# A strided slice copied by three DMA queues: which batches go through on-chip memory first

## The chip, the cores and the metric

The kernel runs on one core of a Trainium2 chip. The metric is the device time of one execution in microseconds. A GB/s here is the bytes that the DMA engines moved per time; a transfer from HBM to HBM counts its bytes once.

## The reference

```python
def setup_inputs():
    batch, seq, dim = 32, 1024, 512
    return {"x": np.random.randn(batch, seq, dim).astype(np.float32),
            "start": 0, "stop": 512, "stride": 2}

def reference(x, start, stop, stride):
    return x[:, start:stop:stride, :].astype(np.float32)
```

Of each of 32 batches the even rows among the first 512 are copied: 256 rows of 512 floats, 2 KB each, 512 KB per batch and 16.78 MB in all. The rows taken from x lie 4 KB apart; in the output they lie one after the other. Nothing is computed, so the kernel is made of DMA transfers alone.

## The kernel before

The 256 output rows of a batch are taken in pairs, which gives two halves of 128 rows each: the even rows (parity 0) and the odd rows (parity 1). One half goes straight from x to the output in HBM, a *direct copy*. The other half is *held*: it is loaded into a tile in SBUF with one row per partition, and stored from there. `apart(b)` gives the parity of the direct half: 1 for the first two batches of every four, 0 for the other two. The held half has the opposite parity.

Transfers are put together as follows.

- A direct copy (line 39) takes two batches, `b` and `b + step`, which have the same parity. It moves 2 x 128 rows, 512 KB. There are 16 of them, in the order of the list `copied`: for each group of eight batches the pairs (0, 5), (2, 7), (1, 4) and (3, 6).
- A load (lines 37 and 42) fills one tile, `held[i]`, with the held halves of batches 2i and 2i+1, again 512 KB. There are 16 tiles, one for each pair of batches, each with its own memory, so no tile is used twice.
- A store (line 46) writes one batch's held half from its tile, 256 KB. There are 32.

Three queues issue them, each in the written order (`manual_schedule`). SP and ACT issue the loads of tiles 0 to 5 in turn, three each (`FIRST = 6`). The gpsimd queue (POOL) issues the 16 direct copies, and after the fourth copy and each one following it one of the loads of tiles 6 to 15, until these are used up. SP then issues all stores. Their order begins with tile 13, the gate: as SP's instructions run in order, no store starts before that tile's load has landed. Tiles 0 to 12, 14 and 15 follow.

Each transfer signals a completion semaphore. The framework gives eight of them to SP and ACT together and eight to the gpsimd queue, in turn. A transfer that takes a semaphore again waits for the one that had it before. So the ninth transfer of the gpsimd queue waits for its first, and SP's stores are at most eight in flight.

Of the kernel before, what the change touches and what calls it, by code (L numbers as in the profile page):

```python
# [3 lines left out]

FIRST = 6


def apart(b):


    return 1 - (b >> 1 & 1)


def two(t, b, step, parity):

    return t[b : b + step + 1 : step].rearrange("b (p two) d -> two p b d", two=2)[parity]


def kernel(tc, x, start, stop, stride, out):

    nc = tc.nc
    src = x[:, start:stop:stride, :]
    B, rows, D = out.shape
    P = rows // 2
    sp, act, pool = nc.sync, nc.scalar, nc.gpsimd  # L30
    copied = [(g + b, step) for g in range(0, B, 8) for b, step in ((0, 5), (2, 5), (1, 3), (3, 3))]
    pairs = B // 2
    with tc.tile_pool(name="io", bufs=1) as io:
        held = [io.tile([P, 2, D], x.dtype, name=f"held{i}") for i in range(pairs)]
        with tc.manual_schedule():
            for i in range(FIRST):
                (sp, act)[i % 2].dma_start(held[i], two(src, 2 * i, 1, 1 - apart(2 * i)))
            for n, (b, step) in enumerate(copied):
                pool.dma_start(two(out, b, step, apart(b)), two(src, b, step, apart(b)))  # L39
                i = n + FIRST // 2  # L40
                if FIRST <= i < pairs:
                    pool.dma_start(held[i], two(src, 2 * i, 1, 1 - apart(2 * i)))  # L42
            order = [pairs - 3, *range(pairs - 3), pairs - 2, pairs - 1]
            for b in (2 * i + k for i in order for k in range(2)):
                to = out[b].rearrange("(p two) d -> two p d", two=2)[1 - apart(b)]
                sp.dma_start(to, held[b // 2][:, b % 2])


# [1 line left out]
_INS = ['x', 'start', 'stop', 'stride']  # L50
_OUTS = [((32, 256, 512), 'float32')]

_NUMBERS = {'start': 0, 'stop': 512, 'stride': 2}


def kernel(**inputs):
    import numpy as _np
    import concourse.bacc as _bacc
    import concourse.tile as _tile
    from concourse import mybir as _mybir  # L60
    from concourse.bass_utils import run_bass_kernel_spmd as _run

    nc = _bacc.Bacc("TRN2", target_bir_lowering=False, num_devices=1)  # L63
    arrays, args = {}, []
    for name in _INS:
        if name in _NUMBERS:
            args.append(_NUMBERS[name])
            continue
        a = _np.ascontiguousarray(inputs[name])
        if a.dtype.kind in "iu":  # L70
            a = a.astype(_np.int64)
        arrays[f"in_{name}_dram"] = a
        args.append(nc.dram_tensor(f"in_{name}_dram", a.shape, _mybir.dt.from_np(a.dtype), kind="ExternalInput").ap())
    for i, (shape, dtype) in enumerate(_OUTS):
        dt = _mybir.dt.from_np(_np.dtype(dtype))
        args.append(nc.dram_tensor(f"out_{i}_dram", shape, dt, kind="ExternalOutput").ap())
    with _tile.TileContext(nc) as tc:  # L77
        kernel(tc, *args)
    r = _run(nc, [arrays], core_ids=[0])
    got = tuple(r.results[0][f"out_{i}_dram"] for i in range(len(_OUTS)))  # L80
    return got[0]
```

## Time and profile before

| | us |
|---|---|
| median of 7 runs | 79.32 (78.46 to 80.31) |
| profiled execution, its own time | 79.26 |
| profiled execution, its span | 77.5 |

| transfers in the profile | count | KB each | issue, engine | issue to landing, median us |
|---|---|---|---|---|
| direct copies | 16 | 512 | POOL, 699 ns | 13.4 |
| loads of tiles 6 to 15 | 10 | 512 | POOL, 728 ns | 13.2 |
| loads of tiles 0, 2, 4 | 3 | 512 | SP | 11.1 |
| loads of tiles 1, 3, 5 | 3 | 512 | ACT | 12.0 |
| stores | 32 | 256 | SP, 0.33 us | 5.9 |

The span runs from the first instruction to the last; the execution's own time holds something before and after it. A transfer's issue is short, and the bytes move later on 16 DMA engines that all queues share. In the profile q0 is the gpsimd queue, q1 SP's and q10 ACT's. The share of a queue is the time that its packets took, in parts of 16 engines' time in the window; with several packets in flight the shares of a short window can add up to a little over 100%.

### The profile page before, as it was taken

How to read it: one execution, taken by the hardware profiler on the slowest of the kernel's cores; microseconds unless marked ns; L12 is line 12 of the kernel's file. 1: busy time of each engine (PE TensorE's matmuls, PEld its weight loads, DVE VectorE, ACT ScalarE, POOL GpSimd, SP SyncE). 2: the span in 40 equal slices, each digit the busy share in tenths (PEclk: the TensorE clock that was granted, in tenths of full speed). 3: DMA queues.
4: the chain of work that ended last, by engine and by line, in shares of the span. 5: the costliest groups of instructions: out<-in, count | busy, mean ns of one | idle time of the engine just before them, and what ended most of it. 6: DMA issues, size and time to landing. Idle time of an engine off the chain costs nothing.

```text
span 77.5 us, 122 instructions
## 1 busy us (share of the span) xinstructions
POOL 18.6 (24%) x30
## 2 busy tenths in 40 slices
POOL 4995003203463355054425100000000000000000
DMA  0899999999999998899999999999999999999940
GB/s 10 256 293 329 314 281 348 300 353 409 383 298 341 362 349 220 294 370 415 376 370 389 330 294 315 337 390 411 404 406 406 363 355 363 349 351 355 340 154 11
DMA packets 9984, 25.17 MB, mean 325 GB/s; under 512 B 1024, under 2 KB 1024, under 8 KB 9984
## 3 DMA queue, kind: packets, MB, share of 16 engines
q0 software_dynamic: 3744, 13.63, 50.2%
q1 hardware_dynamic: 5424, 9.96, 37.7%
q10 hardware_dynamic: 816, 1.57, 6.6%
HBM read 16.78 MB, written 16.78 MB: 433 GB/s over the span
## 4 chain that ended last, share of the span: by engine, by line
DMA 50%; issue 3%; POOLq 1%; POOL 1%; PEldq 0%
DMA held<-in_x_dram 37%; DMA out_dram<-in_x_dram 13%; POOLq L77 1%; POOL out_dram L39 1%; PEldq L77 0%
## 5 line engine op out<-in xcount | busy, mean ns | idle before, releaser
L39 POOL DMA_DIRECT2D out_dram<-in_x_dram x16 | 11.2, 699 | 12.1 <-DMA out_dram<-in_x_dram 9.6
L42 POOL DMA_DIRECT2D held<-in_x_dram x10 | 7.3, 728 | 12.0 <-DMA out_dram<-in_x_dram 7.5
L63 POOL MEMSET const-float32-0.0<- 128x1 f32 x1 | 0.1, 98 | 0.2 <-issue 0.2
L63 POOL MEMSET const-bfloat16-1.0<- 128x1 bf16 x1 | 0.1, 101 | 0.0
L63 POOL MEMSET const-float32-1.0<- 128x1 f32 x1 | 0.1, 98 | 0.0
L63 POOL MEMSET const-uint8-127<- 128x1 uint8 x1 | 0.1, 98 | 0.0
## 6 DMA issues: line engine op xcount, KB each, us to landing
out_dram<-in_x_dram POOLq DMA_DIRECT2D x16, 512.0 KB, 13.4
out_dram<-held SPq DMA_DIRECT2D x32, 256.0 KB, 5.9
held<-in_x_dram POOLq DMA_DIRECT2D x10, 512.0 KB, 13.2
held<-in_x_dram SPq DMA_DIRECT2D x3, 512.0 KB, 11.1
held<-in_x_dram ACTq DMA_DIRECT2D x3, 512.0 KB, 12.0
```

What stands on the lines that cost most here:

```text
L39: pool.dma_start(two(out, b, step, apart(b)), two(src, b, step, apart(b)))
L42: pool.dma_start(held[i], two(src, 2 * i, 1, 1 - apart(2 * i)))
L63: nc = _bacc.Bacc("TRN2", target_bir_lowering=False, num_devices=1)
L77: with _tile.TileContext(nc) as tc:
```

## The change

SP and ACT now load the first two batches of every four, a tile with 256 KB from each of them: SP takes the even batch, ACT the odd one. These are tiles 0, 2, 4 and so on to 14, all of parity 0, eight loads on each queue. The gpsimd queue starts with the eight direct copies of the other two batches of every four, also of parity 0 (the list `last`). Then it loads an odd tile and makes a direct copy from the list `first` in turn, eight times, all of parity 1. The gate of the stores is tile 11 (`gate = B - 10` is batch 22). The stores go on with tiles 0 to 10, 12 and 14, and end with 13 and 15. The stores' size, the direct copies' size and the number of both stay.

```diff
-FIRST = 6
...
+def one(t, b, parity):
+    return t[b].rearrange("(p two) d -> two p d", two=2)[parity]
...
-    copied = [(g + b, step) for g in range(0, B, 8) for b, step in ((0, 5), (2, 5), (1, 3), (3, 3))]
-    pairs = B // 2
+    first = [(g + b, step) for g in range(0, B, 8) for b, step in ((0, 5), (1, 3))]
+    last = [(g + b, step) for g in range(0, B, 8) for b, step in ((2, 5), (3, 3))]
...
+        def direct(b, step):
+            pool.dma_start(two(out, b, step, apart(b)), two(src, b, step, apart(b)))
+
+        def store(b):
+            sp.dma_start(one(out, b, 1 - apart(b)), held[b // 2][:, b % 2])
+
         with tc.manual_schedule():
-            for i in range(FIRST):
-                (sp, act)[i % 2].dma_start(held[i], two(src, 2 * i, 1, 1 - apart(2 * i)))
-            for n, (b, step) in enumerate(copied):
-                pool.dma_start(two(out, b, step, apart(b)), two(src, b, step, apart(b)))
-                i = n + FIRST // 2
-                if FIRST <= i < pairs:
-                    pool.dma_start(held[i], two(src, 2 * i, 1, 1 - apart(2 * i)))
-            order = [pairs - 3, *range(pairs - 3), pairs - 2, pairs - 1]
-            for b in (2 * i + k for i in order for k in range(2)):
-                to = out[b].rearrange("(p two) d -> two p d", two=2)[1 - apart(b)]
-                sp.dma_start(to, held[b // 2][:, b % 2])
+            for b in range(0, B, 4):
+                for k, queue in enumerate((sp, act)):
+                    queue.dma_start(held[b // 2][:, k], one(src, b + k, 1 - apart(b)))
+            for b, step in last:
+                direct(b, step)
+            for n, (b, step) in enumerate(first):
+                pool.dma_start(held[2 * n + 1], two(src, 4 * n + 2, 1, 1 - apart(4 * n + 2)))
+                direct(b, step)
+            gate = B - 10
+            order = [b for b in range(B) if b // 2 % 2 == 0 or b < gate]
+            order = [gate, gate + 1, *order]
+            for b in [*order, *(b for b in range(B) if b not in order)]:
+                store(b)
```

## The prediction

> **What bounds the kernel now.** No engine computes here. The page's busy rows come first, then its DMA queues, and only the queues carry the time.
>
> ```profile
> span 77.5 us, 122 instructions
> POOL 18.6 (24%) x30
> DMA  0899999999999998899999999999999999999940
> DMA packets 9984, 25.17 MB, mean 325 GB/s; under 512 B 1024, under 2 KB 1024, under 8 KB 9984
> q0 software_dynamic: 3744, 13.63, 50.2%
> q1 hardware_dynamic: 5424, 9.96, 37.7%
> q10 hardware_dynamic: 816, 1.57, 6.6%
> HBM read 16.78 MB, written 16.78 MB: 433 GB/s over the span
> ```
>
> The 16 DMA engines are nine tenths busy from the second slice to the second last; the three queue shares add up to 94.5%. So the time is bytes over rate, and the question is at which rate each stage moves. q0 is the gpsimd queue, q1 SP's, q10 ACT's. Second, the chain and SP's waits give the one order that binds:
>
> ```profile
> SPq L46 <- DMA held<-in_x_dram: 41.2, 1, 41.2
> SPq L46 <- DMA out_dram<-held: 14.8, 24, 3.3
> 43.37 28.21 SPq L46 DMA_DIRECT2D out_dram<-held  x32
> ```
>
> SP sits 41.2 us until held13, the gate, has landed; then it stores, eight in flight. Third, stage windows (the columns are: window, length, POOL busy, clock, DMA share, GB/s), cut where queues start or run out:
>
> ```profile
> 0.00:6.00 6.00, 4.93 (x11) 1.00 0.65 188
> 6.00:19.00 13.00, 2.98 (x5) 1.00 1.00 332
> 19.00:48.00 29.00, 10.71 (x16) 1.00 0.99 341
> 48.00:52.00 4.00, 0.00 (x0) 1.00 1.04 369
> 52.00:60.00 8.00, 0.00 (x0) 1.00 1.03 401
> 60.00:77.50 17.50, 0.00 (x0) 1.00 0.87 293
> ```
>
> Stage 1 is start-up with SP's and ACT's loads alone, stage 2 all three queues, stage 3 the gpsimd queue alone (its packets are 99% of it), stage 4 (48 to 60) stores beside its remainder, then a few us of stores alone, stage 5 stores alone with the tail. The first stores are issued at 43.4, but the queue view has 13 packets of q1 before 48. The bytes by queue in stages 2 and 3:
>
> ```profile
> q0 software_dynamic: 624, 2.30, 48.1%
> q10 hardware_dynamic: 553, 1.05, 26.3%
> q1 hardware_dynamic: 503, 0.96, 26.0%
> ...
> q0 software_dynamic: 2710, 9.88, 98.5%
> q1 hardware_dynamic: 13, 0.03, 0.2%
> ```
>
> **What the Trainium skill says.** DMA: Bandwidth & Descriptors, "Issuing engines are not separate DMA queues": queues share the same 16 engines, so spreading transfers gains only issue time. The trace agrees: shares 48.1, 26.3 and 26.0% in stage 2, sum 100%, at 332 GB/s against 341 for one queue. The same page, "Queues, rings and completion order": each engine goes round its queues packet by packet. Take off 16 small completion packets per DMA: q0's 26 DMAs leave 3328 packets for 13.63 MB, 4 KB each; q10's three leave 768 for 1.57 MB, 2 KB each. One turn each would then give gpsimd half the bytes: it had 2.30 of 4.31 MB. The same page, "Latency and other measured facts", has HBM copies that slow down at large power-of-two row pitches (half the rate at 4 MiB), and infers, unverified, that the rows then fall on the same channels. It lists pitches from 512 KiB up; the rows of one transfer here are 8 KB apart in x and 4 KB in out, and this trace has no stage where all transfers share a row half. So it says only that addresses can matter, and stays a rival.
>
> A last set of windows, in the same columns, shows how uneven a stage is inside, which the sums and rivals below need:
>
> ```profile
> 8.00:13.00 5.00, 0.73 (x1) 1.00 0.98 302
> 27.00:28.50 1.50, 0.73 (x1) 1.00 1.06 412
> 28.50:31.00 2.50, 1.42 (x2) 1.00 0.79 215
> 35.00:37.00 2.00, 0.83 (x2) 1.00 1.02 416
> 60.00:73.00 13.00, 0.00 (x0) 1.00 1.06 357
> ```
>
> The gpsimd queue alone can run at 412 to 416, and loses that in holes such as the third line, while stores alone run evenly at 357.
>
> **The change part by part.** Bytes stay: 8.39 MB direct, 8.39 loaded, 8.39 stored, 25.17 in all.
>
> (1) Two loads of 512 KB (1.05 MB) leave the gpsimd queue (24 DMAs, 12.58 MB) for SP and ACT, which load 16 x 256 KB = 4.19 MB instead of 3.15. Price by packet: q10's 6.6% x 77.5 x 16 = 82 us over 768 packets is 107 ns per 2 KB row; q0's 50.2% is 622 us over 3328, 187 ns per 4 KB, 94 per row. 512 rows x 13 ns / 16 engines = +0.4 us. This is a check on the sum below and not added to it.
>
> (2) Issue: SP and ACT issue eight instructions each instead of three, 0.33 us apiece by the stores' row, 2.7 us in all, beside 20 us of their own transfers: nothing. Loads five to eight of each queue wait for a completion semaphore, shared eight among both queues. Behind ACT's waits stands nothing; behind SP's stand the stores, which wait for the gate anyway. Four loads in flight per queue are 1.05 MB at about 78 GB/s per queue, 13 us of work, so the queue doesn't run dry. Eight more DMAs are 128 more completion packets, 8 per engine, under 0.1 us.
>
> (3) POOL now issues eight directs first, then load and direct in turn, each with the same wait for the DMA eight places before. Its instructions, 0.69 and 0.73 us, fall by two, in an engine 24% busy: nothing.
>
> (4) The gate is held11 instead of held13, but it is the nineteenth DMA of the gpsimd queue in both (eight directs, then load and direct five times, then this load; before: eleven directs and eight loads). Stores so flow when that queue has moved the same bytes: 2.30 + 9.88 = 12.18 MB at the point where stage 3 ends.
>
> (5) Stages. 1: unchanged, 6.0 us, 1.13 MB. 2: SP and ACT have 4.19 - 1.13 = 3.06 MB left, at 2.01 MB per 13 us: 19.8 us, to 25.8; gpsimd moves 2.30/13 x 19.8 = 3.50 MB beside it. 3: 12.18 - 3.50 = 8.68 MB at 341: 25.5 us, to 51.3 instead of 48. Left for gpsimd: 0.40 MB instead of 1.45. 4: in before 1.45 + 3.23 MB of stores at 391 (4.69 MB in 12 us). If the first 3.23 MB of stores keep that rate: 3.63 MB, 9.3 us, to 60.6, and the rest as before takes 17.5: 78.1, so +0.6. If the fast part ends instead with the gpsimd queue plus 4.5 us, as in before (its last packets come near 55.5): 1.6 us of mix, 4.5 us at 401, to 57.4 with 2.0 MB stored; stage 5 then has 6.39 MB instead of 5.14, and 1.25 MB at the steady 357 (60 to 73) is 3.5 us: 78.4, so +0.9. I take the middle, +0.75.
>
> (6) Cover at the gate. For some 4.6 us after the gate the stores hardly flow, and gpsimd covers it, with seven DMAs behind the gate in before, five now. By the sum 0.40 MB, about 1.2 us, is left when they flow; but the 16 engines are not level, so some may be dry earlier. Bounds 0 and +1.0 us, a gain excluded because less cover can't help; I take +0.25.
>
> Sum: +1.0 us. The profiled execution took 79.26 with a span of 77.5, so 1.76 lies around it, unchanged; 79.26 + 1.0 = 80.3. The median of the runs, 79.32, is the same to 0.1%.
>
> **The rivals.**
>
> A. Nothing to measure: bytes over rate, the same 16 engines; 79.3. For it: stages 2 and 3 differ by 3% in rate. Against: stores alone run at 357, while every window after 48 with gpsimd beside them is at 369 or more.
>
> B. Faster: the holes of stage 3 go. In before its windows range from 416 down to 215 GB/s. There loads and directs of both row halves follow each other. In the changed kernel every load and direct of stage 3 touches the second half of each row pair only (held of batches 2 and 3 of four, direct of 0 and 1), and of stage 2 the first only. If mixing the halves makes the holes, half of them gone is 375 GB/s: 8.68 MB in 23.1 instead of 25.5, -2.3, so 78.0. It wins by over 1% from 367 GB/s on. Against: holes come at a few places while the mixing is everywhere.
>
> C. Much slower, by the same addresses: with one row half in use, reads and writes fall on fewer paths. At 302 GB/s, the rate of the weakest long stretch (8 to 13 us), stages 2 and 3 with 15.24 MB take 50.5 instead of 45.3 us: +5.2, 85.2 with (5) and half of (6). For it: HBM moves one and a half bytes per queue byte in these stages, some 510 GB/s, the highest in the kernel. Against: every single DMA in before uses one half already, and gpsimd reaches 416.
>
> **How the numbers follow.** Chances: forecast 0.50, A 0.20, B 0.13, C 0.17. About 1% (78.5 to 80.1) is what a measurement can tell from no change. Of the forecast's half, 0.40 lies over 80.1 and 0.09 within; of A 0.14 within, 0.03 on either side; with C 0.60 slower, 0.23 within and B with the rest 0.17 faster. The range goes from half a gain of B, 78.2, to the middle of C, 83.5; the forecast's own range is 79.5 to 81.5.
>
> **What would show it.** Right: ACT's and SP's loads lasting to 24 to 28 us, the gate near 46.7 instead of 43.4, stage 3 at 330 to 355 GB/s, gpsimd empty by 53, and stores alone at about 357 for over 20 us. B is seen in a stage 3 over 365, C in stages 2 and 3 under 315. An idle stretch of the DMA row after the gate shows (6) too small. The prediction is wrong if stage 3's rate moves by over 5% either way, or if stores alone run at 400.

## The result: slower by 0.7%, and the profile after

The changed kernel takes 79.78 us in the median of 27 runs against 79.10 for 64 runs of the kernel before. The ratio of the two, which leaves out the slow runs of each (those over 1.5% above its fastest), is 1.0072, with a 95% interval of 1.0048 to 1.0097. That is +0.57 us (0.38 to 0.77), where +1.0 was forecast. It is clear of zero and under the 1% named as what a measurement can tell, so it falls in the "within 1%" class, not in the "slower" one that had the largest chance.

The profiled execution took 79.15 us, 0.6 below its median, while that of before, 79.26, lay 0.2 above its own. The two spans are therefore all but equal (77.4 and 77.5), and what follows reads rates, byte counts and the order of events from the profiles, and differences of time from the timed runs alone. The page after, its queues:

```profile
span 77.4 us, 128 instructions
DMA packets 10368, 25.17 MB, mean 325 GB/s; under 512 B 1152, under 2 KB 1152, under 8 KB 10368
q0 software_dynamic: 3456, 12.58, 48.3%
q1 hardware_dynamic: 5760, 10.49, 41.3%
q10 hardware_dynamic: 1152, 2.10, 7.2%
```

The bytes moved as the change says: 1.05 MB left q0, half of it for SP, half for ACT. The shares add up to 96.8% (94.5% before): the engines are as full as they were. SP's waits (us in total, times, longest) and its line of stores (start, length):

```profile
SPq L45 <- DMA held<-in_x_dram: 33.1, 2, 28.1
SPq L50 <- DMA held<-in_x_dram: 8.7, 4, 3.0
45.97 25.45 SPq L45 DMA_DIRECT2D out_dram<-held  x32
```

The first line holds the wait for the gate. The second is new: SP's loads five to eight wait for a semaphore. The third shows that no store was late by it, since stores start at 45.97 behind the gate in any case. The stage windows (window, length, POOL busy, clock, DMA share, GB/s), cut where this kernel's queues start or run out, and below the bytes by queue from 50 to 54:

```profile
6.00:25.00 19.00, 4.43 (x7) 1.00 1.04 332
25.00:50.00 25.00, 7.79 (x11) 1.00 0.99 339
50.00:54.00 4.00, 0.00 (x0) 1.00 1.02 385
54.00:60.00 6.00, 0.00 (x0) 1.00 1.06 401
60.00:73.00 13.00, 0.00 (x0) 1.00 1.07 355
...
q0 software_dynamic: 250, 0.89, 59.7%
q1 hardware_dynamic: 347, 0.65, 41.9%
```

All three queues together run at 332 GB/s and gpsimd alone at 339, the rates of before (332 and 341). The stage with three queues lasts six microseconds longer. The first 13 us of it, the stretch that it had in before, read 319. When the stores begin to flow, near 50, gpsimd has 0.92 MB left (0.89, and 0.03 after 54), against 1.45 MB at the same point of before.

### The profile page after: what moved, and what is told of

Its sections match the earlier page's. It is cut to its first block, busy times and chain, and to the rows that moved or that the text cites. A ratio compares the mean times of both kernels' runs of the same rounds, so it can differ in the third digit from the quotient of the medians.

```text
span 77.4 us, 128 instructions
## 1 busy us (share of the span) xinstructions
POOL 17.1 (22%) x28
## 3 DMA queue, kind: packets, MB, share of 16 engines
q0 software_dynamic: 3456, 12.58, 48.3%
## 4 chain that ended last, share of the span: by engine, by line
DMA 43%; POOL 6%; issue 4%; POOLq 1%; PEldq 0%
DMA out_dram<-in_x_dram 30%; DMA held<-in_x_dram 13%; POOL out_dram L42 5%; POOL held L54 1%; POOLq L89 1%; PEldq L89 0%
## 5 line engine op out<-in xcount | busy, mean ns | idle before, releaser
L54 POOL DMA_DIRECT2D held<-in_x_dram x8 | 5.8, 728 | 12.4 <-DMA out_dram<-in_x_dram 10.2
```

The costliest lines, as they stand in the source:

```text
L54: pool.dma_start(held[2 * n + 1], two(src, 4 * n + 2, 1, 1 - apart(4 * n + 2)))
```

## The experiments

Each ratio is to the kernel before on the same chip. The chips differ a little: the median of before was 79.19 beside the first four kernels, and 79.75, 79.63 and 79.64 beside the later ones.

**Which part of the change costs: the bytes, their order, or their size.** The first kernel moves the bytes and leaves the order and the size as in before. Its gate keeps the nineteenth place on the gpsimd queue, so five transfers lie behind it instead of seven:

```diff
-FIRST = 6
+FIRST = 8
-                i = n + FIRST // 2
+                i = n + FIRST // 2 - 1
-            order = [pairs - 3, *range(pairs - 3), pairs - 2, pairs - 1]
+            order = [pairs - 2, *range(pairs - 2), pairs - 1]
```

> Before, with tiles 6 and 7 moved from the gpsimd queue to SP and ACT (eight loads of 512 KB there instead of six), the gate again at the nineteenth place of the gpsimd queue (tile 14), row halves mixed as in before. Theory 1, the moved 1.05 MB: slower by the whole of what the change cost, +0.5 to +0.9 us, ratio 1.006 to 1.011. Theory 2, the order by row halves: within 0.25 us of before. Theory 3, the loads of 256 KB with their waits: within 0.25 us of before.

Measured: 1.0054 (1.0025 to 1.0084), +0.43 us. The second kernel changes the order (of loads, copies and stores) and nothing else:

```diff
-    copied = [(g + b, step) for g in range(0, B, 8) for b, step in ((0, 5), (2, 5), (1, 3), (3, 3))]
+    copied = [(g + b, step) for half in (((2, 5), (3, 3)), ((0, 5), (1, 3))) for g in range(0, B, 8) for b, step in half]
+    tiles = [0, 2, 4, 6, 8, 10, 12, 14, 1, 3, 5, 7, 9, 11, 13, 15]
...
-                (sp, act)[i % 2].dma_start(held[i], two(src, 2 * i, 1, 1 - apart(2 * i)))
+                j = tiles[i]
+                (sp, act)[i % 2].dma_start(held[j], two(src, 2 * j, 1, 1 - apart(2 * j)))
...
-                    pool.dma_start(held[i], two(src, 2 * i, 1, 1 - apart(2 * i)))
-            order = [pairs - 3, *range(pairs - 3), pairs - 2, pairs - 1]
+                    j = tiles[i]
+                    pool.dma_start(held[j], two(src, 2 * j, 1, 1 - apart(2 * j)))
+            order = [11, *range(11), 12, 14, 13, 15]
```

> Before, with the same number and size of transfers on each queue, but ordered by row half: SP and ACT load tiles 0, 2, 4, 6, 8, 10, the gpsimd queue makes the direct copies of half 0 first and then those of half 1, and loads tiles 12, 14 and then the odd ones. Gate tile 11 at the nineteenth place. Theory 1, the moved bytes: within 0.25 us of before. Theory 2, the order by row halves: +0.5 to +0.9 us. Theory 3, the 256 KB loads: within 0.25 us.

Measured: 1.0014 (0.9988 to 1.0040), nothing that can be told from before. The third takes the changed kernel and gives SP and ACT whole tiles:

```diff
-            for b in range(0, B, 4):
-                for k, queue in enumerate((sp, act)):
-                    queue.dma_start(held[b // 2][:, k], one(src, b + k, 1 - apart(b)))
+            for k, b in enumerate(range(0, B, 4)):
+                (sp, act)[k % 2].dma_start(held[b // 2], two(src, b, 1, 1 - apart(b)))
```

> After, with SP's and ACT's loads as whole tiles of 512 KB, four each in turn, instead of half tiles of 256 KB, eight each; so no load there waits for a semaphore. Theory 1 and theory 2: as slow as after, ratio 1.005 to 1.010 to before. Theory 3, the 256 KB loads and their waits cost it: back to before, ratio 0.998 to 1.003.

Measured: 1.0049 (1.0011 to 1.0086): not back at before. Nothing shows that the smaller loads and their waits cost, though the interval leaves room for a part. Theory 1 stands: the moved bytes carry 0.43 of the 0.57 us, and the rest is inside the intervals. That five transfers behind the gate cost anything by themselves is not seen below, where before has five with no byte moved.

**The dose.** If bytes on SP and ACT cost, twice as many should cost twice as much. Ten loads there (`FIRST = 10`, `i = n + FIRST // 2 - 4`, gate tile 14):

> The dose doubled: before with ten loads of 512 KB on SP and ACT instead of six (2.1 MB moved instead of 1.05), gate again at the nineteenth place of the gpsimd queue (tile 14), three transfers behind it. If each moved MB costs what the first did (+0.43 us per 1.05 MB by the run with eight): ratio 1.008 to 1.014. If only a loss that the first step brought counts, and no price per byte: 1.003 to 1.007.

Measured: 1.0119 (1.0077 to 1.0160), +0.95 us; the second step costs what the first did. Four loads (`FIRST = 4`, `i = n + FIRST // 2 + 1`, gate tile 12):

> The dose taken the other way: before with four loads on SP and ACT instead of six, so 1.05 MB more on the gpsimd queue, gate at its nineteenth place (tile 12), nine transfers behind it. If bytes on the gpsimd queue are cheaper, faster than before: ratio 0.993 to 0.998. If before stands at the best point between two costs (too little gpsimd work beside the stores on one side, too long a gpsimd queue on the other): 1.000 to 1.008.

Measured: 1.0047 (1.0020 to 1.0075). So it isn't a price per byte that goes on in both directions: six loads are the best of four, six, eight and ten, and the change walks one step away from it. The profiles don't show where the time goes. The windows from 6 to 40 us, before any store, of the kernels with six loads, six with a later gate (tile 14, below), eight, ten and four:

```profile
6.00:40.00 34.00, 12.32 (x18) 1.00 0.99 340
6.00:40.00 34.00, 12.33 (x18) 1.00 1.00 333
6.00:40.00 34.00, 11.48 (x17) 1.00 1.01 342
6.00:40.00 34.00, 9.72 (x15) 1.00 1.00 328
6.00:40.00 34.00, 13.16 (x19) 1.00 1.01 332
```

Up to 40 us the first two kernels issue the same transfers in the same order, and still differ by 2%. In the same way the changed kernel reads 340 and its variant with larger stores (below) 329. So a step of 2% or 3% between two of these profiles need not come from the dose; the dose rests on the timed runs.

**The place of the gate.** In the changed kernel, tile 9 (`gate = B - 14`), then tile 5 (`gate = B - 22`):

> After, with the gate two places earlier on the gpsimd queue (tile 9, the seventeenth of 24), so that seven of its transfers lie behind the gate as in before, instead of five; tile 11 is stored late. Theory 1a, the moved loads are dearer per byte on SP and ACT: still 1.004 to 1.008 to before. Theory 1b, the loss is that fewer gpsimd transfers lie beside the stores: back to 0.998 to 1.002.

Measured: 1.0025 (0.9995 to 1.0055).

> After, with the gate at tile 5 (the thirteenth of 24 on the gpsimd queue), so that eleven of its transfers lie beside the stores. If stores beside gpsimd transfers are the cheaper place for them, as the gate at tile 9 hints: at or under before, ratio 0.994 to 1.002, and a longer stretch at 380 to 400 GB/s. If an earlier gate only makes reads and stores meet earlier: 1.002 or more, and the stretch after the gate stays under 350.

Measured: 1.0106 (1.0060 to 1.0153), with 328 GB/s from 41 to 56 us, where loads, copies and stores meet. In the kernel before, tile 14 and then tile 12 as the first of `order`:

> Before, with the gate one tile later (tile 14, the twenty-first of 26), so that five gpsimd transfers lie behind it as in after, instead of seven. Theory 1a: within 0.25 us of before. Theory 1b: 1.004 to 1.008, with no load moved.

Measured: 1.0007 (0.9973 to 1.0041).

> Before, with the gate one tile earlier (tile 12, the seventeenth of 26), nine gpsimd transfers behind it. After gained from such a step (1.0072 to 1.0025). If the best place is the seventeenth in both kernels: 0.994 to 0.998. If what counts is seven transfers behind the gate, which before has already: 1.000 to 1.006.

Measured: 1.0010 (0.9983 to 1.0037). Around its place the gate is flat in before. In the changed kernel the ratio for tile 9 points to a gain of 0.4 us, but the intervals of 1.0025 and 1.0072 overlap, and the medians of all runs, 80.34 against 79.75 for before, show no gain. So theory 1b, fewer gpsimd transfers beside the stores, is neither shown nor excluded; five transfers behind the gate cost nothing measurable where no load was moved. An early gate does harm.

**Loads by themselves.** Three kernels with the 16 loads alone (`FIRST = 16`), no direct copies, and the stores of tile 15 only. The first loads on SP and ACT in turn. The second loads on gpsimd:

```diff
-                (sp, act)[i % 2].dma_start(held[i], two(src, 2 * i, 1, 1 - apart(2 * i)))
+                pool.dma_start(held[i], two(src, 2 * i, 1, 1 - apart(2 * i)))
```

The third loads on gpsimd in loads of one batch, 256 KB:

```diff
-                (sp, act)[i % 2].dma_start(held[i], two(src, 2 * i, 1, 1 - apart(2 * i)))
+                for k in range(2):
+                    half = src[2 * i + k].rearrange("(p two) d -> two p d", two=2)
+                    pool.dma_start(held[i][:, k], half[1 - apart(2 * i)])
```

> Only the 16 loads of 512 KB, in turn on SP and ACT, and the two stores of the last tile (the rest of the output is left out). If a load on these queues is dearer by itself, as the 107 ns per 2 KB row in before hint: 290 to 330 GB/s in the steady stretch. If it is dear only beside the direct copies: 380 to 430 GB/s.

> The same 16 loads of 512 KB and two stores, all loads on the gpsimd queue (the rest of the output is left out). If the queue makes the price: 380 to 430 GB/s here against 290 to 330 on SP and ACT. If loads of this kind cost the same on every queue by themselves: within 5% of the rate on SP and ACT.

> The same bytes on the gpsimd queue as 32 loads of one batch, 256 KB each (the rest of the output is left out). If packets of 4 KB make gpsimd loads cheap and packets of 2 KB dear, and these loads go in packets of 2 KB: the rate falls to that of SP and ACT, 290 to 330 GB/s. If the size of the packet does not matter: as with 512 KB, within 5%.

Measured, in one run of each, the window from 5 to 25 us, in this order:

```profile
5.00:25.00 20.00, 0.00 (x0) 1.00 1.01 331
5.00:25.00 20.00, 7.89 (x11) 1.00 1.00 324
5.00:25.00 20.00, 13.29 (x26) 1.00 0.99 319
```

Alone, a load costs the same on every queue within 4%. The third kernel's packets are still of 4 KB (8.39 MB in 2560 packets less 512 small ones), so it doesn't test the size of the packet. SP's and ACT's queues are by themselves not dearer.

**The stores, and where the rows lie.** Whole tiles per store:

```diff
-            sp.dma_start(one(out, b, 1 - apart(b)), held[b // 2][:, b % 2])
+            if b % 2 == 0:
+                sp.dma_start(two(out, b, 1, 1 - apart(b)), held[b // 2])
```

> After, with the stores as whole tiles of 512 KB, 16 instead of 32, still eight in flight, so twice the bytes. If the 357 GB/s of stores alone are set by how many bytes are in flight, stores alone rise to about 395 and 1.5 us go (ratio to before about 0.988). If they are set by where the rows lie in HBM, stores alone stay at 350 to 360 and the time stays that of after, 1.004 to 1.010.

Measured: 1.0088 (1.0049 to 1.0126), stores alone at 356 GB/s from 60 to 73 us: twice the bytes in flight left the rate where it was. Then all direct copies of half 1 and everything held of half 0:

```diff
 def apart(b):
-    return 1 - (b >> 1 & 1)
+    return 1
```

> After, with apart(b) = 1 for every batch: every load and store is of row half 0 and every direct copy of half 1, so that both halves are in use in every stage until only stores are left. Theory 1 and theory 3: as slow as after, ratio 1.005 to 1.010. Theory 2, one half at a time costs: ratio 0.997 to 1.003. If stores of one half alone are slower than stores that alternate, the store-only stretch falls under 350 GB/s and the ratio rises over 1.010 instead.

Measured: 1.1433 (1.1320 to 1.1547), 11 us slower, which no theory had. Its windows, in the loading stage and in the stores:

```profile
8.00:32.00 24.00, 2.94 (x5) 1.00 0.97 221
72.00:86.00 14.00, 0.00 (x0) 1.00 1.03 391
```

Loading falls to 221 GB/s from 332, and stores alone rise to 391 from 355. The next kernel flips the halves for the upper 16 batches and stores from lower and upper tiles in turn:

```diff
-    return 1 - (b >> 1 & 1)
+    return 1 - ((b >> 1 ^ b >> 4) & 1)
...
-            order = [b for b in range(B) if b // 2 % 2 == 0 or b < gate]
-            order = [gate, gate + 1, *order]
+            high, low = (11, 8, 9, 10, 12, 14, 13, 15), range(8)
+            order = [2 * i + k for pair in zip(high, low) for k in range(2) for i in pair]
```

> After, with the parity of the halves flipped for batches 16 to 31 (apart(b) takes b >> 1 xor b >> 4), and the stores taken in turn from tiles of the lower and the upper 16 batches, gate tile 11 still first. If what matters is parity xor bit 1 of the batch (one group of rows is held, the other copied directly, and the two run beside each other), loads and direct copies still meet across the groups, and stores now alternate between both: stores alone at 385 to 400 GB/s instead of 357, 1.3 to 1.8 us less than after, ratio to before 0.983 to 0.992. If parity itself or the order alone matters, stores alone stay at 350 to 365 and the ratio is 1.004 to 1.010; if the groups collide in the loading stages, these fall under 320 GB/s and the ratio is over 1.01.

Measured: 1.1215 (1.1179 to 1.1250). The stores alone rose (last line), the loading stages collided (second and fourth):

```profile
12.00:16.00 4.00, 1.42 (x2) 1.00 1.04 393
20.00:36.00 16.00, 2.84 (x4) 1.00 0.97 200
36.00:44.00 8.00, 3.46 (x5) 1.00 1.00 335
48.00:60.00 12.00, 1.42 (x2) 1.00 0.96 227
70.00:82.00 12.00, 0.00 (x0) 1.00 1.05 404
```

The collapses come where gpsimd's order of copies reaches batches 16 to 31, which it does twice. What they share with the first eight copies of the kernel above is that the copied half has the parity of bit 1 of the batch. So the copies were run alone, with no loads and stores, in an order that has eight of this kind first and eight of the other kind last:

> Only the direct copies, no loads and no stores (the held half of the output is left out), with apart(b) = 1 for every batch. The first eight copies are of batches 2 and 3 of every four, where parity 1 equals bit 1 of the batch; the last eight are of batches 0 and 1 of every four, where it differs, as for all copies in before. If a copy of the first kind is slow by itself (its own read and write meet in HBM): about 200 to 260 GB/s in the first half, 340 to 420 in the second. If it was slow only beside loads: both halves equal, 340 to 420.

Measured:

```profile
8.00:26.00 18.00, 4.14 (x6) 1.00 0.91 156
34.00:41.00 7.00, 0.00 (x0) 1.00 0.96 356
```

A copy of the first kind is slow by itself, below half the speed of the other; it needs no load beside it. This is what `apart(b)` avoids in the kernels before and after, where every direct copy is of the second kind.

## Why the prediction was partly right, and which step failed

**Right.** Slower, and by the moved bytes: the run that moves them alone has 0.43 of the 0.57 us. The course came near what was worked out: SP's and ACT's loads end near 25.4 (25.8 in the sum), the gate falls at 45.97 (46.7), gpsimd alone runs at 339 (341), stores alone at 355 (357). The costs set at nothing in (2) and (3) can't be told from nothing: whole tiles in place of half ones gave 1.0049 beside 1.0072, and order alone 1.0014.

**The step that failed: the size of the terms in (5) and (6).** The sum had +0.75 for the stages and +0.25 for the lost cover. The timed runs have +0.57 for both, so it charged 0.43 us too much (0.2 to 0.6).

- Step (6) priced a hole after the gate at 0.25. In the four microseconds after the gate, before and after read:

```profile
43.37:47.37 4.00, 0.00 (x0) 1.00 1.00 317
45.97:49.97 4.00, 0.00 (x0) 1.00 0.96 320
```

The share of busy time is lower in the changed kernel, but the bytes are the same: this pair shows no loss. Timed, five transfers behind the gate in before cost 0.06 us, between -0.2 and +0.3. Other single profiles with five behind it read from 269 (before with gate 14) to 331 (the changed kernel with whole tiles loaded), so nothing bounds the term more closely than the timing.

- Step (5) took the middle of two accounts of the fast stores. By the first, all but the last 5.14 MB, which is 20.03 MB, are moved by 60.6 us. The profile has 20.04 MB by then (before: 20.03 by 60.0), with 3.05 MB stored by 60.0, where the fast rate ends. The first account's +0.6 would have been the number to take; the middle added 0.15.
- Step (4) let the stores flow once gpsimd had moved 12.18 MB, as in before, with 0.40 MB left. They flowed with 0.92 MB left: the time from gate to flow was the same four microseconds, but gpsimd had moved fewer bytes, and its queue was empty near 55, not by 53. At 385 (50 to 54) instead of 339 GB/s the 0.52 MB are 0.2 us that the kernel did not pay. A first stage and a stage 3 slightly under their forecast (1.10 MB and 339 GB/s instead of 1.13 and 341) cost it about as much again, so this error hardly shows at 60.6.

With the first account and no hole the sum is +0.6, as timed. That this is the right split is likely and not shown. It leans on one profile of each kernel, and the end of these two differs by as much as the effect:

```profile
73.00:77.50 4.50, 0.00 (x0) 1.00 0.31 111
73.00:77.50 4.50, 0.00 (x0) 1.00 0.49 162
```

At 73 us before (first line) had 0.50 MB left and the changed kernel 0.73, yet both ended near 77.4. The 16 engines end less evenly in the profile of before: a store's sixteen parts land 3.1 us apart (mean of the last eight stores), against 1.6 in the changed kernel. So the spans came out equal although the changed kernel was behind at 60 us. Whether that is chance or regular stays open. And as the sum works with stage rates 3% apart (332 and 341) from a single profile, while kernels with the same transfers differ by as much, it is partly luck that the first account came out to a tenth of a microsecond.

**The check in (1) agreed for the wrong reason.** It gave +0.4 us from 107 ns per row on ACT's queue against 94 on gpsimd's, and the run with the bytes alone gave 0.43. But 94 is a mean over loads and direct copies, and loads alone cost the same on each queue (331 and 324 GB/s). On the changed kernel's own page the order even turns round: q10's 7.2% are 89 us over 1024 rows, 87 ns each, and q0's 48.3% are 598 us over 3072 packets of two rows, 97 ns a row. The price is not in the queue. What remains as a cause is that the stage with three queues is longer and the stage of stores beside gpsimd shorter. The runs do not separate these two. The rate of the stage with three queues doesn't settle it: from 6 to 19 us it is 332 in before and 319 in the changed kernel, but also 318 in before with gate 14, which issues the same transfers there as before does.

**The rivals.** A, bytes over rate, is excluded by the interval of the change, though by little. B and C both fell: with one row half at a time, stage 3 had the rate of before (339 against 341; the page's slices there go from 276 to 392 GB/s, in before from 220 to 415), and order alone changed nothing. C's thought that addresses decide holds in another place: what matters is not which half is in use, but which half of which batch is copied directly.

## What to carry to other kernels

Where the DMA engines are full before and after, as here, ask which stages a change of queues makes longer or shorter and at which rate each moves; and look for the balance point in both directions, as six loads were better than four and eight. Before a difference of rates between two profiles is read as an effect, compare two kernels that issue the same transfers: here they differ by 2 to 3%, more than the whole change. A packet's mean time on a queue is a price only for the mix that this queue carried: compare like transfers, alone if need be. For copies from HBM to HBM, run the copies by themselves with both choices of address before the rest is tuned around them.

## What the runs showed of the hardware that was not expected

- The direct copies run at 156 GB/s where the parity of the row equals bit 1 of the batch and at 356 where it differs. In the output that is bit 11 against bit 20 of the offset (rows of 2 KB, batches of 512 KB); which addresses meet in HBM, source and target or two others, was not tried.
- Stores alone run at 355 to 357 GB/s in before and after, where all rows stored have the parity of bit 1 of their batch, and at 391 and 404 where stores of both kinds alternate. Twice the bytes in flight left 356. Why the first 3 MB of stores reach 401 in before and after, up to about 60 us, stays open.
- In before and after, the stores' bytes begin to flow some four microseconds after their issue, while the gpsimd queue still has transfers to move. In the kernels with loads alone, where nothing else was in flight any more, the two stores had landed 2.2 us after their issue. What sets the four microseconds was not tried.
- The 16 engines do not end together: in before a store's sixteen parts land about 3 us apart near the end of the kernel.
